# Expert rounds of 32 slots over all columns, with the third round in a TensorE branch

## The chip, the cores and the metric

One core of a Trainium2 chip runs the whole kernel as one program. The metric is the device time of that core in microseconds, and of several runs the median counts. TensorE does the matmuls (its sequencer fetches, waits and branches), VectorE (DVE), ScalarE (ACT) and GpSimd (POOL) work on rows of tiles, SyncE (SP) mostly issues DMAs; 16 DMA engines move the data for all of them.

## The reference

One decoder layer for 512 prompt tokens and 32 sample tokens (544 in all, `d_model` 1024, float32): a gated convolution and a forgetting attention, merged by sigmoid gates, a layer norm, then a routed mixture of 16 experts and a second layer norm. Only the mixture matters here:

```python
gl = (t @ w_group)                       # 4 groups, the best one is taken
el = (t @ w_router)                      # 4 experts in each group
top_w, top_i = lax.top_k(softmax(el of the best group), 2)
ids = g_idx * 4 + top_i                  # two experts a token
for e in range(16):
    h = silu(t @ w1[e]) * (t @ w3[e])    # 1024 -> 512
    y = y + gate[:, e:e + 1] * (h @ w2[e])   # 512 -> 1024
x = layer_norm(ALPHA * x + y)
```

Each of the 544 tokens goes to two experts, so an expert has 68 tokens on average.

## The kernel before, in words

The kernel first computes the two branches and the first layer norm, writes the normed rows to `x1d` in HBM, ranks the router's logits and gives every token a slot in its two experts' lists (L1078 to L1084). An expert has `CAP` = 96 slots; a block behind `tc.If(top > CAP)` (L1527), skipped here, does the rest if a list is longer.

**Weights.** All 16 experts' weights stream from HBM through a ring of 20 places of 1 MB (`RING`, `raw_load`, L778): per expert four `we` tiles (j = 0 to 3, each two rows k of w1 and of w3, two DMAs of 512 KB) and two `wd` tiles (j = 4, 5, each half of w2, one DMA). Nearly all are issued by SP's queue, in the order of use: up(e) first half, up(e) second half, down(e-1), up(e+1) and so on. From the 21st on, a load also waits until the tile five places before it has landed (L807 to L811, `AHEAD` = 5).

**One expert.** `place` (L1109) compares slots with list positions and takes token numbers and gates out by five matmuls, `gather` (L1119) fetches up to 96 rows of `x1d` by an indirect DMA on POOL. `x_t` (L1208) transposes them on VectorE, 12 instructions of 32x256 elements (expert 0 uses TensorE instead). `up` (L1229) forms x @ w1 and x @ w3, `glu` (L1238) the silu product, `h_t` (L1245) transposes h by 16 VectorE instructions of 32x96, `down` (L1266) forms h @ w2, scales by the gate (one ScalarE operation for columns 0 to 767, three of VectorE for the rest) and adds the rows into `acc` in HBM by an indirect DMA on POOL (L1279). For the last two experts (`E0` = 14 on) `down_kept` keeps y in SBUF instead and TensorE adds it at the end.

**How the matmuls are packed.** The stationary operand of a matmul is 32 slots, a quarter of TensorE's columns, so four matmuls run side by side in the four column groups q:

```python
for s in range(3):
    for q in range(4):
        g, c = (q, s) if q < 3 else (s, 3)
        mm(out(q, s), lhs(k, g), rhs(c), start=k == 0 and s != 1, ...)
```

g is a group of 32 slots, c a quarter of the output columns: column group q < 3 holds slots 32q to 32q+31 and quarters 0 to 2 in turn, group 3 holds quarter 3 of all slots. A *round* is one s: four matmuls of 256 moving columns. Up has 8 values of k with three rounds each, down 4.

**Order.** In the loop at L1318 the program order is up(e) first half, h_t(e-1), x_t(e+1), up(e) second half, place and gather of e+4, down(e-1), glu(e). Two double banks of PSUM alternate between up's and down's results. Before it (L1138 to L1196): lists of experts 0 and 1 and their gathers, then the arithmetic of the gates on VectorE, with matmuls on constants (`keep_warm`) that fill TensorE's gaps. After it: the residual rows are loaded from `x1d` by SP and `acc` is added onto them by POOL (L1357 to L1374), TensorE adds the kept experts (`z_part`), and the second layer norm follows in an order written out by hand (`TAIL`).

Of the kernel before, what the change touches and what calls it, by code (L numbers as in the profile page):

```python
# [33 lines left out]
NT = 5  # L34
# [54 lines left out]
def layer_kernel(ctx: ExitStack, tc: tile.TileContext, i_, o_):  # L89
# [18 lines left out]
    w1 = i_["w1"].rearrange("l e (p k) c -> p (l e) k c", p=128)  # L108
    w3 = i_["w3"].rearrange("l e (p k) c -> p (l e) k c", p=128)
# [839 lines left out]
    wk = []  # L949

    def parts_of(x, n, cm=None):
# [5 lines left out]
        if (x, n) == (NT - 1, 1):  # L957
            wk.append(ps_mm("wake")[:, 0])
            keep_warm(wk[0], WK[0])
# [120 lines left out]
    mm(pps[:, :NT * NE], before, asf.rearrange(flat), start=False, stop=True, skip_group_check=True)  # L1080
    keep_warm(wk[0], WK[3])
# [7 lines left out]
    gat3 = small("gat3", [NE, 3])  # L1089
# [50 lines left out]
    keep_warm(wk[0], WK[4])  # L1140

# [60 lines left out]
    def packed_mm(out, lhs, rhs, k, last):  # L1202
        for s in range(3):
            for q in range(4):
                g, c = (q, s) if q < 3 else (s, 3)
                mm(out(q, s), lhs(k, g), rhs(c), start=k == 0 and s != 1, stop=k == last, skip_group_check=True)  # L1206

    def x_t(e):  # L1208
        x = p2.tile([128, 8, CAP], F32, name="xgT", tag=("xgh", "xgl")[e % 2], bufs=1)
        if e:  # L1210
            rows = xgs[e % NXG].rearrange("c (p k) -> c k p", k=8)
            for g in range(3):
                for j in range(4):
                    nc.vector.transpose(x[32 * j:32 * j + 32, :, 32 * g:32 * g + 32],  # L1214
                                        rows[32 * g:32 * g + 32, :, 32 * j:32 * j + 32])
            return x
        for q in range(2):
            pp = (ps_t if q == 0 else ps_o)("xgT")
            for k in range(4):
                nc.tensor.transpose(pp[:, k, :CAP], xgs[e % NXG].rearrange("c (p k) -> c k p", k=8)[:CAP, 4 * q + k],  # L1220
                                    ident[:CAP, :CAP])
# [6 lines left out]

    def up(e, a, pab, x):  # L1229
        flat = pab.rearrange("p a b -> p (a b)")  # L1230
        for j in (2 * a, 2 * a + 1):
            raw = raw_e(e, j)
            for kk in range(2):
                packed_mm(lambda q, s: flat[32 * q:32 * q + 32, 256 * s:256 * s + 256].rearrange("p (a b) -> p a b", a=2),
                          lambda k, g: x[:, k, 32 * g:32 * g + 32],
                          lambda c: raw[:, :, kk, 128 * c:128 * c + 128], 2 * j + kk, 7)
# [8 lines left out]
    def h_t(su, tag="hh"):  # L1245
        h = p2.tile([128, 4, CAP], F32, name="hT", tag=tag, bufs=1)
        if tag == "hh":
            h3 = h[:, 3].rearrange("p (g c) -> p g c", g=3)
            for q in range(4):
                for j in range(4):  # L1250
                    ps = slice(32 * j, 32 * j + 32)
                    nc.vector.transpose(h[ps, :3, 32 * q:32 * q + 32] if q < 3 else h3[ps],  # L1252
                                        su[32 * q:32 * q + 32, :, 32 * j:32 * j + 32])
            return h
        pp = ps_t("hT")
        for k in range(3):
            nc.tensor.transpose(pp[:, k], su[:, k], ident)
        h_done.append((nc.scalar.activation(h[:, :3], pp[:, :3, :CAP], AF.Copy),
                       nc.vector.tensor_copy(h[:, 3].rearrange("p (g c) -> p g c", g=3), pp[:, :3, CAP:])))
# [5 lines left out]

    def down(e, h):  # L1266
        y = p2.tile([CAP, D], F32, name="y", tag="y", bufs=YB)
        py = ps_mm("py").rearrange("p a b -> p (a b)")
        for j in range(2):
            raw = raw_e(e, 4 + j)  # L1270
            for kk in range(2):
                packed_mm(lambda q, s: py[32 * q:32 * q + 32, 256 * s:256 * s + 256],
                          lambda k, g: h[:, k, 32 * g:32 * g + 32],
                          lambda c: raw[:, kk, 256 * c:256 * c + 256], 2 * j + kk, 3)
        nc.scalar.activation(y[:, :768], py[:CAP, :768], AF.Copy, scale=gat[:CAP, e:e + 1])  # L1275
        for s in range(3):
            nc.vector.tensor_scalar(y[32 * s:32 * s + 32, 768:], py[96:, 256 * s:256 * s + 256], gat3[96:, e, s:s + 1],
                                    None, op0=ALU.mult)
# [39 lines left out]
    for e in range(NE):  # L1318
        pab = ps_mm("pab")
# [22 lines left out]
        if e == NE - 1:  # L1342
            su = glu(pab)
            ht2 = h_t(su, "hl")
            with tc.issue_after(h_done[-1][0].ins):
# [181 lines left out]
    with tc.If(top > CAP):  # L1527
# [17 lines left out]
        with tc.For_i(0, NE, 1) as e:  # L1545
# [3 lines left out]
            for w in (w1, w3):  # L1549
                wt = halves_of("wt", [128, 1, 4, 512])  # L1550
                for a in range(2):
                    nc.sync.dma_start(wt[a], w[:, bass.ds(e, 1), 4 * a:4 * a + 4])
# [6 lines left out]
            for t in range(NT):  # L1559
# [4 lines left out]
                for q in range(2):  # L1564
                    pp = ps_t("xoT")
                    for k in range(4):
                        nc.tensor.transpose(pp[:, k, :m], xt.rearrange("c (p k) -> c k p", k=8)[:m, 4 * q + k],
# [3 lines left out]
                for i in range(2):  # L1571
                    for k in range(8):
                        mm(pab[:m, i], xT[:, k, :m], wup[i][k // 4][:, 0, k % 4], start=k == 0, stop=k == 7)
# [56 lines left out]
```

## Time and profile before

| | us |
|---|---|
| median of 3 runs | 770.4 (769.72 to 771.73) |
| the profiled execution, its own time | 777.0 |
| its span, first to last instruction | 775.3 |
| TensorE busy | 729.9 (94%) |
| VectorE busy | 478.8 (62%) |
| ScalarE busy | 200.6 (26%) |
| the expert stage, first up matmul to last down product | 471.6 to 745.8 |

The rows below come from the profiled execution, so terms of a sum are set against its 777.0 us. A line gives a start and a length in us, or for a group of instructions the busy time and the mean of one in ns; a name like pab<-we,xgT is the tile written and the tiles read, and Lnnn the line of the kernel. After an arrow stands what ended a wait.

### The profile page before, as it was taken

Reading aid. Unit: us, or ns where it says so; the run is one execution under the profiler, and the core shown is the slowest. Engines: PE = TensorE matmul, PEld = TensorE weight load, DVE = VectorE, ACT = ScalarE, POOL = GpSimd, SP = SyncE. Lnnn points to the kernel's source line nnn. Section 1 sums busy time; section 2 is a strip of 40 time slices with the busy share of each in tenths; the row PEclk is TensorE's granted clock in tenths of the full one; section 3 lists DMA queues with packets and bytes.
Section 4 is the critical chain, followed back from the end, with each engine's and each line's share of the span. In section 5 each row is a group of like instructions: output and inputs, shape, how many; then the busy total and the mean of one; then the engine's idle time right before and its main releaser. Section 6 shows DMA issues by size and latency. Waiting matters only on the chain.

```text
span 775.3 us, 18856 instructions
## 1 busy us (share of the span) xinstructions
PE 729.9 (94%) x8105; PEld 560.3 (72%) x8105; DVE 478.8 (62%) x1148; ACT 200.6 (26%) x360; POOL 131.7 (17%) x170
## 2 busy tenths in 40 slices
PE   7799999999999999999999977989999999999990
PEld 5599888899797999999976734545555555566550
DVE  3333766763345222333555776699999999986457
ACT  3343556534145222222424320001000010001132
POOL 5411000013441000000020531011111111100134
PEclk8899999999999999999999997999999999999995
DMA  9545411126543434434175697999999999999853
GB/s 231 168 151 183 129 59 56 59 65 208 163 119 106 163 114 158 164 109 164 55 278 213 191 411 233 332 343 354 358 367 361 342 357 346 351 377 362 318 119 117
DMA packets 65433, 169.66 MB, mean 219 GB/s; under 512 B 6145, under 2 KB 26673, under 8 KB 65345
## 3 DMA queue, kind: packets, MB, share of 16 engines
q1 hardware_dynamic: 54928, 137.93, 50.1%
q0 software_dynamic: 9552, 27.84, 13.3%
q10 hardware_dynamic: 864, 2.62, 0.9%
q8 instruction: 66, 1.08, 0.6%
q14 instruction: 23, 0.18, 0.1%
HBM read 157.40 MB, written 14.49 MB: 222 GB/s over the span
## 4 chain that ended last, share of the span: by engine, by line
PE 84%; DVE 7%; DMA 5%; issue 2%; ACT 1%; SPq 0%; DVEq 0%; another core or an unknown queue 0%; POOLq 0%; ACTq 0%
PE pab L1206 17%; PE pj L169 10%; PE pj L171 9%; PE pj L170 9%; PE py L1206 9%; DVE xgT L1214 3%; DMA xg<-x1d,gix 2%; PE py L171 2%; PE py L170 2%; PE py L169 2%; PE py L1288 2%; PE po L170 2%; PE po L171 2%; PE po L169 2%; PE S L567 1%
## 5 line engine op out<-in xcount | busy, mean ns | idle before, releaser
L1206 PE MATMUL pab<-we,xgT 128*32 128x256 f32 x3072 | 173.6, 385 | 4.8 <-DVE su L1242 4.8
L1206 PEld LDWEIGHTS pab<-we,xgT 128*32 128x32 f32 x3072 | 100.4, 112 | 73.7 <-DVE su L1242 5.3
L1214 DVE STREAM_TRANSPOSE xgT<-xg 32x256 f32<-32x256 f32 x180 | 115.7, 643 | 12.2 <-DMA xg<-x1d,gix 6.8
L1206 PE MATMUL py<-wd,hT 128*32 128x256 f32 x1344 | 76.6, 380 | 0.2 <-DVE hT L1252 0.2
L169 PE MATMUL pj<-xth,wgas 128*128 128x272 f32 x256 | 73.9, 288 | 0.0
L170 PE MATMUL pj<-xtl,wgas 128*128 128x272 f32 x256 | 73.8, 288 | 0.0
L171 PE MATMUL pj<-xth,wgas 128*128 128x272 f32 x256 | 73.6, 288 | 0.0
L165 DVE TENSOR_TENSOR wgas<-wga,wgas 128x1024 fp32r<-128x1024 f32 x16 | 19.6, 1226 | 85.6 <-ACT wgas L164 85.6
L1252 DVE STREAM_TRANSPOSE hT<-su 32x96 f32<-32x96 f32 x240 | 64.7, 269 | 7.9 <-PE py L1206 4.1
L1206 PEld LDWEIGHTS py<-wd,hT 128*32 128x32 f32 x1344 | 42.8, 110 | 28.3 <-DVE hT L1252 1.2
L1241 ACT ACTIVATE su<-pab 128x384 f32<-128x384 f32 x16 | 7.8, 490 | 170.8 <-DVE hT L1252 113.6
L169 PEld LDWEIGHTS pj<-xth,wgas 128*128 128x128 f32 x256 | 48.2, 188 | 0.8 <-issue 0.8
L170 PEld LDWEIGHTS pj<-xtl,wgas 128*128 128x128 f32 x256 | 48.1, 188 | 0.0
L171 PEld LDWEIGHTS pj<-xth,wgas 128*128 128x128 f32 x256 | 48.1, 188 | 0.0
L1279 POOL DMA_INDIRECT acc<-y,gix x14 | 20.1, 1434 | 163.2 <-DVE hT L1252 152.4
L169 PE MATMUL pj<-xth,wqks 128*128 128x272 f32 x128 | 38.6, 302 | 0.0
L171 PE MATMUL pj<-xth,wqks 128*128 128x272 f32 x128 | 36.9, 288 | 0.0
L170 PE MATMUL pj<-xtl,wqks 128*128 128x272 f32 x128 | 36.9, 288 | 0.0
L164 ACT ACTIVATE wgas<-wga 128x1024 fp32r<-128x1024 f32 x16 | 16.9, 1055 | 45.0 <-DMA wga<-in_w_in_dram 44.2
L1275 ACT ACTIVATE y<-py,gat 96x768 f32<-96x768 f32 x14 | 12.5, 896 | 60.8 <-PE py L1206 60.8
L170 PE MATMUL po<-wos,mxh 128*128 128x512 f32 x64 | 26.0, 406 | 0.4 <-DVE wos L165 0.4
L169 PE MATMUL po<-wos,mxl 128*128 128x512 f32 x64 | 25.5, 402 | 0.0
(442 smaller groups left out, 1553.5 us busy)
## 6 DMA issues: line engine op xcount, KB each, us to landing
we<-in_w_dram SPq DMA_DIRECT2D x124, 512.0 KB
wd<-in_w_dram SPq DMA_DIRECT2D x31, 1024.0 KB
wga<-in_w_in_dram SPq DMA_DIRECT2D x8, 1024.0 KB
wqk<-in_w_in_dram SPq DMA_DIRECT2D x4, 1024.0 KB
wo<-in_w_o_dram SPq DMA_DIRECT2D x4, 1024.0 KB
xa<-in_x_prompt_dram SPq DMA_DIRECT2D x4, 512.0 KB
ckb<-cdr POOLq DMA_DIRECT2D x8, 256.0 KB
wcg<-in_w_in_dram SPq DMA_DIRECT2D x2, 1024.0 KB
```

The source lines that it names most:

```text
L164: nc.scalar.activation(h, src, AF.Copy)
L165: (eng or nc.vector).tensor_sub(l, src, h.bitcast(F32))
L169: mm(out, al, bh, start=first, stop=False)
L170: mm(out, ah, bl, start=False, stop=False)
L171: return mm(out, ah, bh, start=False, stop=last)
L1206: mm(out(q, s), lhs(k, g), rhs(c), start=k == 0 and s != 1, stop=k == last, skip_group_check=True)
L1214: nc.vector.transpose(x[32 * j:32 * j + 32, :, 32 * g:32 * g + 32], rows[32 * g:32 * g + 32, :, 32 * j:32 * j + 32])
L1241: nc.scalar.activation(su, ab[:, :, 0], AF.Silu)
L1252: nc.vector.transpose(h[ps, :3, 32 * q:32 * q + 32] if q < 3 else h3[ps], su[32 * q:32 * q + 32, :, 32 * j:32 * j + 32])
L1275: nc.scalar.activation(y[:, :768], py[:CAP, :768], AF.Copy, scale=gat[:CAP, e:e + 1])
L1279: nc.gpsimd.indirect_dma_start(out=acc, out_offset=bass.IndirectOffsetOnAxis(ap=gix[:CAP, e:e + 1], axis=0), in_=y, in_offset=None, bounds ...
L1288: pe_last.append(mm(py[:CAP], h[:, k], raws[k // 2][:, k % 2, n * 512:(n + 1) * 512], start=k == 0, stop=k == 3))
```

## The change

Slots are taken in three rounds of 32 (g = 0, 1, 2), and in a round the four column groups hold the four quarters of the up columns. The quarters are interleaved in blocks of 32 columns, so that one VectorE transpose by 32x32 blocks turns h over whole. Down has its four column groups hold slots 0 to 63 in two halves of the columns (rounds 0 and 1) or slots 64 to 95 in four quarters (round 2). For experts 0 to 13 the third round stands in a branch of TensorE on a bit that says whether the expert has more than 64 tokens; the bits are counted by five matmuls, packed by VectorE and loaded into a register of TensorE. Both PSUM banks become lasting tiles, and ScalarE sets the third round's columns of up to zero once. The y scalings all go to ScalarE, w1 and w3 are cut so that a piece is contiguous in HBM, and x's rows are taken in the matching order. The overflow block is adapted and otherwise as before.

```diff
-    w1 = i_["w1"].rearrange("l e (p k) c -> p (l e) k c", p=128)
+    w1 = i_["w1"].rearrange("l e (j p r) c -> p (l e) j r c", p=128, r=2)
...
-            return [2, 2, 512], [(w[:, e, 2 * j:2 * j + 2], i) for i, w in enumerate((w1, w3))]
+            return [2, 2, 512], [(w[:, e, j], i) for i, w in enumerate((w1, w3))]
...
+    full = ps_s("full")
+    for x in range(NT):
+        mm(full[:, :NE], onesb, asf[:, x], start=x == 0, stop=x == NT - 1)
     keep_warm(wk[0], WK[3])
...
         if e < E0:
-            for s in range(3):
-                nc.vector.tensor_copy(gat3[96:, e, s:s + 1], gat[32 * s:32 * s + 32, e:e + 1])
+            nc.scalar.activation(gat2[64:, e, 0:1], gat[:64, e:e + 1], AF.Copy)
+            for q in range(4):
+                nc.scalar.activation(gat2[32 * q:32 * q + 32, e, 1:2], gat[64:96, e:e + 1], AF.Copy)
...
     second = place_early(1)[1]
     keep_warm(wk[0], WK[4])
+    bits = p2.tile([1, NE], F32, name="bits")
+    many = p2.tile([1, 2], F32, name="many")
+    manyi = p2.tile([1, 1], I32, name="manyi")
+    for e in range(NE):
+        nc.gpsimd.memset(bits[:, e:e + 1], float(2 ** e))
+    nc.vector.scalar_tensor_tensor(bits, full[:1, :NE], 64.0, bits, op0=ALU.is_gt, op1=ALU.mult,
+                                   accum_out=many[:, 0:1])
+    nc.vector.tensor_copy(manyi, many[:, 0:1])
+    third_of = nc.values_load(manyi[:1, 0:1], engines=[mybir.EngineType.PE], min_val=0, max_val=2 ** NE - 1)
...
+    def rows_by_two(xr):
+        return xr.rearrange("c (j p r) -> c j r p", p=128, r=2)
...
-                    nc.vector.transpose(x[32 * j:32 * j + 32, :, 32 * g:32 * g + 32],
-                                        rows[32 * g:32 * g + 32, :, 32 * j:32 * j + 32])
+                    nc.vector.transpose(x[32 * j:32 * j + 32, :, 32 * g:32 * g + 32].rearrange("p (j r) s -> p j r s", r=2),
+                                        rows[32 * g:32 * g + 32, :, :, 32 * j:32 * j + 32])
...
+    def up_round(g, pab, x, raws, ks):
+        out = pab.rearrange("p a b -> p (a b)")[:, 256 * g:256 * g + 256].rearrange("p (a b f) -> p a b f", a=2, f=32)
+        for k in ks:
+            rhs = raws[k // 2][:, :, k % 2].rearrange("p a (b c f) -> p a b c f", c=4, f=32)
+            for c in range(4):
+                mm(out[32 * c:32 * c + 32], x[:, k, 32 * g:32 * g + 32], rhs[:, :, :, c], start=k == 0 and g != 1,
+                   stop=k == 7, skip_group_check=True)
+    banks.append(ps_mm("moe"))
+    for b in banks:
+        nc.scalar.activation(b[:, 1, :256], ident.unsqueeze(1).to_broadcast([128, 2, 128]), AF.Copy, scale=0.0)
...
+    def third(e):
+        return tc.If((third_of >> e) & 1 > 0) if e < E0 else ExitStack()
     def up(e, a, pab, x):
-        for j in (2 * a, 2 * a + 1):
-            raw = raw_e(e, j)
-            for kk in range(2):
-                packed_mm(..., 2 * j + kk, 7)
+        raws = {}
+        ks = range(4 * a, 4 * a + 4)
+        for k in ks:
+            if k % 2 == 0:
+                raws[k // 2] = raw_e(e, k // 2)
+            for g in range(2):
+                up_round(g, pab, x, raws, (k,))
+        with third(e):
+            up_round(2, pab, x, raws, ks)
...
     def h_t(su, tag="hh"):
         h = p2.tile([128, 4, CAP], F32, name="hT", tag=tag, bufs=1)
-        if tag == "hh":
-            h3 = h[:, 3].rearrange("p (g c) -> p g c", g=3)
-            for q in range(4):
-                for j in range(4):
-                    ...
-        pp = ps_t("hT")
-        for k in range(3):
-            nc.tensor.transpose(pp[:, k], su[:, k], ident)
+        h_done.append(nc.vector.transpose(h.rearrange("p b (g s) -> p g b s", g=3),
+                                          su.rearrange("p g (b f) -> p g b f", b=4)))
+        return h
...
+    def down_round(r, py, h, raws, ks):
+        for k in ks:
             for q in range(4):
+                g, c = (q % 2, 2 * (q // 2) + r) if r < 2 else (2, q)
+                mm(py[32 * q:32 * q + 32, 256 * r:256 * r + 256], h[:, k, 32 * g:32 * g + 32],
+                   raws[k // 2][:, k % 2, 256 * c:256 * c + 256], start=k == 0 and r != 1, stop=k == 3,
+                   skip_group_check=True)
     def down(e, h):
+        for j in range(2):
+            raws[j] = raw_e(e, 4 + j)
+            for k in (2 * j, 2 * j + 1):
+                for r in range(2):
+                    down_round(r, py, h, raws, (k,))
+        with third(e):
+            down_round(2, py, h, raws, range(4))
-        nc.scalar.activation(y[:, :768], py[:CAP, :768], AF.Copy, scale=gat[:CAP, e:e + 1])
-        for s in range(3):
-            nc.vector.tensor_scalar(y[32 * s:32 * s + 32, 768:], py[96:, 256 * s:256 * s + 256], gat3[96:, e, s:s + 1],
-                                    None, op0=ALU.mult)
+        nc.scalar.activation(y[:64, :512], py[:64, :512], AF.Copy, scale=gat[:64, e:e + 1])
+        nc.scalar.activation(y[:64, 512:], py[64:, :512], AF.Copy, scale=gat2[64:, e, 0:1])
+        for q in range(4):
+            nc.scalar.activation(y[64:, 256 * q:256 * q + 256], py[32 * q:32 * q + 32, 512:768], AF.Copy,
+                                 scale=gat2[32 * q:32 * q + 32, e, 1:2])
...
     for e in range(NE):
-        pab = ps_mm("pab")
+        pab = bank()
```

## Rows read from the trace of the kernel before

**Rows 1.** The chain of waits, 540 to 600: start, us, what

```profile
552.45 5.32 PE py L1206 x96
557.76 10.36 PE pab L1206 x192
568.12 0.32 PE pmt L1113 x5
```

**Rows 2.** Windows: busy us of PE, PEld, DVE, ACT, POOL; PEclk, DMA share, GB/s

```profile
440.00:460.00 20.00, 18.39 (x116) 10.56 (x114) 15.57 (x55) 5.55 (x9) 6.53 (x5) 1.00 0.99 374
...
480.00:500.00 20.00, 19.95 (x362) 11.67 (x358) 12.56 (x44) 0.98 (x2) 3.43 (x3) 1.00 1.03 334
500.00:550.00 50.00, 45.00 (x782) 25.57 (x778) 48.39 (x117) 3.67 (x5) 5.91 (x5) 0.97 1.00 355
550.00:600.00 50.00, 50.00 (x919) 29.71 (x911) 48.13 (x125) 4.16 (x6) 8.41 (x7) 1.00 1.01 361
```

**Rows 3.** Waits of SP's queue, 472 to 550: us, times, longest

```profile
SPq L805 <- PE pab L1206: 28.9, 12, 8.4
SPq L805 <- PE pmt L1113: 24.6, 4, 17.8
SPq L805 <- PE py L1206: 11.4, 5, 3.3
```

**Rows 4.** Waits of SP's queue, 550 to 718

```profile
SPq L805 <- DMA we<-in_w_dram: 78.6, 38, 4.7
SPq L805 <- DMA wd<-in_w_dram: 44.2, 17, 5.0
SPq L805 <- PE pab L1206: 1.4, 4, 0.4
```

**Rows 5.** Timeline of SP's queue, 712 to 725: start, us, instructions

```profile
713.84 4.54 SPq L805 DMA_DIRECT2D wd<-in_w_dram  x2
718.49 3.62 SPq L1365 DMA_DIRECT2D z<-x1d  x3
```

**Rows 6.** Timeline, 735 to 746: start, us, instructions, idle before

```profile
736.34 0.91 POOL L1374 DMA_DIRECT2D z<-acc  x1 [13.95 <-DMA z<-x1d]
...
738.64 4.46 PE L1288 MATMUL py<-wd,hT 128*96 128x512 f32 x10
...
744.23 0.67 DVE L1426 SCALAR_TENSOR_TENSOR z<-z,pz 128x512 f32<-128x512 f32 x1
```

**Rows 7.** Timeline, 460 to 525

```profile
461.41 1.06 POOL L1120 DMA_INDIRECT xg<-x1d,gix  x1 [6.11 <-DVE pg L1162]
...
471.57 7.76 PE L1206 MATMUL pab<-we,xgT 128*32 128x256 f32 x96
...
507.13 12.23 PE L1206 MATMUL pab<-we,xgT 128*32 128x256 f32 x192 [4.84 <-DVE su L1242]
```

**Rows 8.** Windows, after TensorE's gap before 507

```profile
507.00:510.50 3.50, 3.37 (x32) 1.58 (x36) 3.37 (x9) 0.00 (x0) 0.85 (x1) 0.52 0.93 371
```

**Rows 9.** One line's instructions: L1352, L1527 (ns min/median/max)

```profile
L1352 PEldq TENSOR_LOAD <-flagi x1: 485/485/485, 751.3 to 751.3; - x1
...
L1527 PEldq COMPARE_BRANCH  x1: 3589/3589/3589, 751.9 to 751.9; - x1
...
L1527 DVEq COMPARE_BRANCH  x1: 76/76/76, 770.9 to 770.9; - x1
```

**Rows 10.** Groups of instructions, 480 to 720: busy us, mean ns, idle

```profile
L1214 DVE STREAM_TRANSPOSE xgT<-xg 32x256 f32<-32x256 f32 x171 | 109.9, 643 | 12.1 <-DMA xg<-x1d,gix 6.8 <-PE pab L1206 2.8
...
L1252 DVE STREAM_TRANSPOSE hT<-su 32x96 f32<-32x96 f32 x232 | 62.5, 269 | 7.8 <-PE py L1206 4.1
...
L1277 DVE TENSOR_SCALAR y<-py,gat 32x256 f32<-32x256 f32 x42 | 20.6, 490 | 0.6
...
L1275 ACT ACTIVATE y<-py,gat 96x768 f32<-96x768 f32 x14 | 12.5, 896 | 60.8 <-PE py L1206 60.8
...
L1241 ACT ACTIVATE su<-pab 128x384 f32<-128x384 f32 x15 | 7.4, 490 | 165.8 <-DVE hT L1252 113.6 <-PE pab L1206 52.2
```

More of the change, by code (lines that the diff above doesn't have):

```diff
@@ L948, in layer_kernel @@
     zt_last = {}
-    wk = []
+    wk, banks = [], []
     def parts_of(x, n, cm=None):
@@ L1088, in layer_kernel @@
     gat = small("gat", [NE])
-    gat3 = small("gat3", [NE, 3])
+    gat2 = small("gat2", [NE, 2])
     gix = small("gix", [NE], I32)
@@ L1196, in layer_kernel @@
     nc.vector.tensor_copy(flagi[:1], flag[:1])
-    def packed_mm(out, lhs, rhs, k, last):
-        for s in range(3):
-            for q in range(4):
-                g, c = (q, s) if q < 3 else (s, 3)
-                mm(out(q, s), lhs(k, g), rhs(c), start=k == 0 and s != 1, stop=k == last, skip_group_check=True)
+    def rows_by_two(xr):
+        return xr.rearrange("c (j p r) -> c j r p", p=128, r=2)
     def x_t(e):
@@ L1219, in x_t @@
             for k in range(4):
-                nc.tensor.transpose(pp[:, k, :CAP], xgs[e % NXG].rearrange("c (p k) -> c k p", k=8)[:CAP, 4 * q + k],
+                nc.tensor.transpose(pp[:, k, :CAP], rows_by_two(xgs[e % NXG])[:CAP, 2 * q + k // 2, k % 2],
                                     ident[:CAP, :CAP])
@@ L1264, in layer_kernel @@
     pe_last = []
+    def down_round(r, py, h, raws, ks):
[5 more added lines that the diff above has]
+                   skip_group_check=True)
     def down(e, h):
         y = p2.tile([CAP, D], F32, name="y", tag="y", bufs=YB)
[L1268 removed]
+        py = bank().rearrange("p a b -> p (a b)")
+        raws = {}
         for j in range(2):
[L1270 to L1274, printed above, removed]
[L1275 to L1278 removed]
+            raws[j] = raw_e(e, 4 + j)
[6 more added lines that the diff above has]
+        nc.scalar.activation(y[:64, 512:], py[64:, :512], AF.Copy, scale=gat2[64:, e, 0:1])
+        for q in range(4):
+            nc.scalar.activation(y[64:, 256 * q:256 * q + 256], py[32 * q:32 * q + 32, 512:768], AF.Copy,
+                                 scale=gat2[32 * q:32 * q + 32, e, 1:2])
         nc.gpsimd.indirect_dma_start(out=acc, out_offset=bass.IndirectOffsetOnAxis(ap=gix[:CAP, e:e + 1], axis=0),
@@ L1344, in layer_kernel @@
             ht2 = h_t(su, "hl")
-            with tc.issue_after(h_done[-1][0].ins):
+            with tc.issue_after(h_done[-1].ins):
                 onehots_t(e)
@@ L1566, in layer_kernel @@
                     for k in range(4):
-                        nc.tensor.transpose(pp[:, k, :m], xt.rearrange("c (p k) -> c k p", k=8)[:m, 4 * q + k],
+                        nc.tensor.transpose(pp[:, k, :m], rows_by_two(xt)[:m, 2 * q + k // 2, k % 2],
                                             ident[:m, :m])
@@ L1572, in layer_kernel @@
                     for k in range(8):
-                        mm(pab[:m, i], xT[:, k, :m], wup[i][k // 4][:, 0, k % 4], start=k == 0, stop=k == 7)
+                        mm(pab[:m, i], xT[:, k, :m], wup[i][k // 4][:, 0, k % 4 // 2, k % 2], start=k == 0, stop=k == 7)
                 su = p2.tile([128, 512], F32, name="suo", tag="su", bufs=1)
```

26 lines of the change are left out of this document (10 added, 16 removed).

## The prediction, made before the changed kernel ran

> **What bounds the kernel now.** The engine table says only who is busy over the span: TensorE most, VectorE next. The chain of waits says where: in the expert stage every piece of it belongs to TensorE, one expert after another [rows 1]. A period is 10.36 (up) + 0.32 (placing) + 5.32 (down) = 16.0 us, with no gap between the pieces. Up is 96 matmuls, recorded as 192 (two passes each), in 24 rounds of four blocks: 10.36 / 24 = 0.432 us a round. Down has 12 rounds.
>
> Behind TensorE stands a second bound, which the windows show: from 480 to 600 the DMA engines are busy 1.00 to 1.03 of the time, at 334 to 361 GB/s [rows 2]. By the code one expert's weights are eight pieces of 512 KB and two of 1024 KB, 6.29 MB. At 355 GB/s they take 17.7 us, more than the 16.0 us in which TensorE uses them up, and gathers and accumulating scatters share the engines. The kernel can do this because the ring has 20 places of 1 MB and is full when the experts begin. The waits of SP's queue show that stock run down: from 472 to 550 weight loads wait for TensorE to free a place (28.9 + 24.6 + 11.4 us) [rows 3], from 550 to 718 for earlier loads to land (78.6 + 44.2 us) and hardly for TensorE (1.4 us in its largest group) [rows 4]. At the end little is left: the last two weight tiles are issued from 713.84 on, the last one just before the transfer at 718.49 [rows 5]. The code lets a load go when the one five tiles before it has landed, so five tiles are under way: 5 x 1.05 MB / 355 GB/s = 14.8 us, and the last lands near 733 (an estimate from these rows). TensorE comes to that tile one block after 738.64, at about 739.5 [rows 6]: the stock is then worth 6.5 us. **TensorE is the bound, and the delivery of weights lies only some 6 us behind it.**
>
> **The change part by part.**
>
> *Rounds left out.* An expert of at most 64 tokens skips slots 64 to 95: 8 of 24 rounds up and 4 of 12 down, 12 x 0.432 = 5.18 us. The reference's router, worked out on its own inputs (seed 0), gives experts 0 to 15 the counts 63 58 79 72 54 64 63 69 67 57 64 58 82 84 69 85. Of the 14 that can branch, 8 skip (0, 1, 4, 5, 6, 9, 10, 11); 2, 3, 7, 8, 12 and 13 keep all rounds behind a branch, 14 and 15 without one. TensorE loses 8 x 5.18 = 41.5 us of work.
>
> *What of this reaches the end.* Little: from 550 on loads already follow one another through full DMA engines [rows 2, 4], and a faster TensorE adds no bytes per second. It waits for weights instead. What moves is the beginning. The first half of expert 0 takes 7.76 us [rows 7]; with 8 of 12 rounds it is over 7.76 / 3 = 2.6 us sooner, and loading, which stood still on a full ring (the longest single wait is 17.8 us [rows 3]), resumes that much earlier. After it, until 550, loads no longer wait for places: 20 us at 334 and 50 us at 355 GB/s go at 361 [rows 2], 20 x (1 - 334/361) + 50 x (1 - 355/361) = 2.3 us. So weights end 4.9 us sooner. The lower bound is 0 (all of it lost to gathers, which then come earlier too), the upper one 4.9 plus the 6.5 us of stock, if the tail follows the last tile.
>
> *The tail.* Since TensorE then waits for the last tile and not the tile for TensorE, up to 6.5 us more can go. But the end needs the residual rows too: POOL, after 13.95 us of waiting for a load, issues the accumulation onto the first of them at 736.34, and VectorE adds to that row at 744.23 [rows 6]. This chain moves with the DMA queue, by 4.9 us, not with TensorE. Its landing stands in no row and lies between the two times, so between 0 and 6.5 us go; I take the middle, 3.3.
>
> *The branches*, three per branching expert, 42. VectorE's taken branch cost 0.076 us; TensorE's only one took 3.589 us, and it jumps over the whole overflow loop [rows 9]. Here 16 matmuls are jumped over. I take 0.1 us, since that distance is nearer to VectorE's, and keep 3.6 for a rival. At 0.1 us, 4 us in all, TensorE's new waiting covers it; without that cover it would count in full.
>
> The Trainium skill's page "Runtime: NRT & Kernel Launch" (section "Instruction fetch mechanics") speaks against this part: a taken branch whose target lies outside the fetched window has to load the target's page first, so control flow at run time is dear. By that rule, should every skip be such a miss, the time would be rival C's. The trace's long TensorE jump agrees with it; no run here shows a short one on TensorE.
>
> *Counting and the register.* Five matmuls of 16 columns (five small ones take 0.32 us [rows 1]), two small VectorE operations (each under the 0.27 us of the smallest transpose [rows 10], 0.5 us in all), 16 one-element memsets on POOL, which waited 6.11 us before the first gather [rows 7], and a register load on TensorE, 0.485 us [rows 9]. TensorE has little but warming matmuls there until the gathered rows land, shortly before its first up matmul at 471.57 [rows 7], so only VectorE's part lies on the way to the gates: +0.5 us. Were the memsets queued behind the gathers, VectorE would stand before the gate arithmetic, with everything behind it on its queue, and TensorE's gate products behind that: up to 2 us, kept for the range.
>
> *VectorE and ScalarE.* The 16 transposes of h (269 ns each, 4.3 us) become one of 128x384: forms of 96 and 256 columns give (643 - 269) / 160 = 2.34 ns a column, 269 + 288 x 2.34 = 943 ns [rows 10]; the upper bound is the 4.3 us of now. Three scalings of y (490 ns) leave VectorE. ScalarE's one of 896 ns becomes six: by the forms of 768 and 384 columns 1.06 ns a column, 2.7 us [rows 10], with five copies of one column more. ScalarE works 4 us in 50 in this stage [rows 2], so it covers this at nothing; if it did not, y's scatter would be late. VectorE is nearly full now (48 of 50 us [rows 2]); without these 4.8 us per expert TensorE's gain could not be used before 550. The 12 transposes of x keep count and size; another stride may make them cheaper, or up to twice as dear (12 x 0.643 = 7.7 us more), which fits into the time that weights take per expert.
>
> *Order of w1 and w3.* Pieces stay as many and 4 KB a row; their place in HBM becomes contiguous, as w2's already is. Taken as 0; the bounds are the 334 and 374 GB/s of neighbouring windows [rows 2].
>
> *Later release.* The third round reads both tiles of a half, so the first is freed with the second. It costs nothing where loads wait for landings, and the 2.6 us at the start already count both as freed together.
>
> **Sum.** 4.9 + 3.3 - 0.5 = 7.7 us. The profiled execution's own time becomes 777.0 - 7.7 = 769.3; that execution is 6.6 us above the median of the runs shown, so against the median it is 770.4 - 7.7 = **762.7 us**.
>
> **The rivals.**
> *A, weights arrive faster.* If the new order of w1 and w3 lets loading run at the 374 GB/s of 440 to 460 rather than 355 [rows 2], 255 us of it shrink by 255 x (1 - 355/374) = 13 us: 750. If delivery were no bound at all, 770.4 - 41.5 = 729. Against it: the DMA engines are full, and the contiguous w2 already is a third of the bytes. 0.08.
> *B, no change.* The gain turns into waiting. The residual rows may be just in time, so that the tail gives nothing; and a TensorE that waits runs slower afterwards: after a gap of 4.84 us [rows 7] the next 3.5 us were granted 0.52 of the clock, 1.2 GHz for most of them [rows 8], which loses 1.7 us of work. Three such gaps near the end take the 4.9 us back: 770. Against it: experts 12 to 15 run all rounds, 16.0 us of work where weights take 17.7 and more, so gaps there are short. 0.17.
> *C, slower: branches stall.* Each skip costs what TensorE's one branch did: 24 x 3.589 = 86 us against the 41.5 saved, 770.4 + 44.6 = 815. It decides from 41.5 / 24 = 1.7 us per skip on. Against it: that branch jumps over a loop many times longer. 0.10.
> *D, it skips nothing*, because the block is entered anyway: 770 to 774. The counts speak against it. 0.03, two parts of three for no change.
>
> **How the numbers follow.** The forecast has 0.62; its own range goes from 756 (4.9 + 6.5, and some faster delivery) to 767 (half the early gain and no tail). What a measurement of this kernel can tell from no change is about 0.3%, 2.3 us. Faster: 0.62 + 0.08 = 0.70; the same: 0.17 + 0.02 = 0.19; slower: 0.10 + 0.01 = 0.11. The range 753 to 773 leaves out C and most of A.
>
> **What would show it.** Right: TensorE's periods of about 11 us for the first skipping experts, and from about expert 10 on gaps before up pieces that weight transfers end; SP's waits for TensorE gone after 480, those for landings there from the start; DMA share 1.0 as before; the last weight tile issued near 713; one h transpose of about 0.9 us. Wrong: branches of microseconds on TensorE, more than 375 GB/s from 500 to 700, or a last tile issued no earlier than now.

## The result, and the profile after

The changed kernel takes 776.1 us in the median of six runs (773.7 to 777.5), the kernel before 770.7 in runs beside them (768.5 to 771.8). The ratio is 1.0070, with a 95% interval of 1.0048 to 1.0092: **slower by 0.7%**, where 1% faster was forecast, and outside the forecast range. The profiled execution takes 775.7 us, with a span of 774.0.

The spans of the two traces, 775.3 before and 774.0 after, do not show the loss, because the profiled execution of the kernel before came late to the expert stage: its first up matmul starts at 471.57 [rows 7], the changed kernel's at 465.84. From there to the end of the last down product it is 274.2 us before and 278.9 after, so times of the two traces are best compared from these starts.

Inside the expert stage the rounds are skipped as forecast. First the page's busy times, then TensorE's timeline:

```profile
PE 701.7 (91%) x7339; PEld 549.8 (71%) x7339; DVE 359.6 (46%) x842; ACT 247.5 (32%) x501; POOL 133.1 (17%) x186
```

```profile
465.84 5.82 PE L1247 MATMUL moe<-we,xgT 128*32 128x256 f32 x64
...
472.36 3.66 PE L1247 MATMUL moe<-we,xgT 128*32 128x256 f32 x64
...
476.49 3.66 PE L1247 MATMUL moe<-we,xgT 128*32 128x256 f32 x64
...
485.73 3.66 PE L1295 MATMUL moe<-wd,hT 128*32 128x256 f32 x64
...
491.67 10.57 PE L1247 MATMUL moe<-we,xgT 128*32 128x256 f32 x192 [2.28 <-DVE su L1278]
```

A half of up without its third round is 64 records and 3.66 us; half of expert 2's 192 records in 10.57 us is 5.3. TensorE's busy time falls from 729.9 to 701.7 us and VectorE's from 478.8 to 359.6. SP's waits between 472 and 550 changed hands too; columns: us, times, longest:

```profile
SPq L805 <- DMA we<-in_w_dram: 33.5, 17, 3.8
SPq L805 <- DMA wd<-in_w_dram: 17.8, 7, 3.9
SPq L805 <- PE pmt L1118: 13.6, 2, 13.4
SPq L805 <- PEq L1271: 6.2, 2, 3.9
```

In [rows 3] TensorE held SP there for 64.9 us; now it is mostly landings. Weights come no faster, as one window shows, first before and then after; the last two columns are DMA share and GB/s:

```profile
500.00:700.00 200.00, 195.00 (x3538) 115.32 (x3534) 190.27 (x470) 16.64 (x24) 28.11 (x23) 0.99 1.00 356
```

```profile
500.00:700.00 200.00, 174.18 (x2968) 109.45 (x2963) 84.06 (x207) 53.02 (x125) 27.74 (x22) 0.98 1.01 356
```

Nor do they come sooner: the four `we` loads of the last up half start 236.5 us after the first up matmul in both (at 708.09 before, at 702.32 after).

The loss is at the end of SP's queue. Its timeline, for comparison with [rows 5], and then the chain of waits:

```profile
702.32 3.39 SPq L805 DMA_DIRECT2D we<-in_w_dram  x4
706.16 4.14 SPq L1401 DMA_DIRECT2D z<-x1d  x3
717.59 0.78 SPq L1408 DMA_DIRECT2D z<-acc  x2
718.43 1.31 SPq L805 DMA_DIRECT2D wd<-in_w_dram  x2
```

```profile
709.64 7.94 DMA acc<-y,gix
717.58 0.02 issue
717.59 0.32 SPq L1408
...
718.95 19.36 DMA wd<-in_w_dram
738.31 0.04 issue
738.36 3.67 PE py L1324 x8
```

Before, the last two weight tiles (wd) were issued ahead of the residual loads. Now five residual loads stand ahead of them, and the fourth reads `acc`: it waits for the last scatter, issued at 709.64 and landed 7.94 us later. From 705.7 to 718.4 no weight load was issued, and the last tile went out at 718.95, 253.1 us after the first up matmul (before: at 718.00, 246.4 us after it). TensorE, which began expert 14's down product 245.2 us after the first up matmul (before: 249.9), waited for both tiles:

```profile
732.16 3.73 PE L1324 MATMUL py<-wd,hT 128*96 128x512 f32 x4 [3.92 <-DMA wd<-in_w_dram]
738.36 3.67 PE L1324 MATMUL py<-wd,hT 128*96 128x512 f32 x8 [2.47 <-DMA wd<-in_w_dram]
...
742.82 1.88 PE L1324 MATMUL py<-wd,hT 128*96 128x512 f32 x4
```

No line of the diff orders these DMAs: in the text of both kernels the residual loads stand ahead of the last two tiles (L1400 and L1489 before, L1436 and L1525 after). Each queue's order is made when the program is built, and it came out differently.

### The profile page after: what moved, and what is told of

It reads as the page before. It is cut to its first block, busy times and chain, and to the rows that moved or that the text cites. A ratio compares the mean times of both kernels' runs of the same rounds, so it can differ in the third digit from the quotient of the medians.

```text
span 774.0 us, 17319 instructions
## 1 busy us (share of the span) xinstructions
PE 701.7 (91%) x7339; PEld 549.8 (71%) x7339; DVE 359.6 (46%) x842; ACT 247.5 (32%) x501; POOL 133.1 (17%) x186
## 5 line engine op out<-in xcount | busy, mean ns | idle before, releaser
L1247 PE MATMUL moe<-we,xgT 128*32 128x256 f32 x2560 | 151.9, 387 | 19.6 <-DMA we<-in_w_dram 11.8
L1247 PEld LDWEIGHTS moe<-we,xgT 128*32 128x32 f32 x2560 | 96.1, 111 | 72.5 <-issue 31.5
L1227 DVE STREAM_TRANSPOSE xgT<-xg 32x256 f32<-32x256 f32 x180 | 78.3, 435 | 109.3 <-PEq L1271 50.4
L1295 PE MATMUL moe<-wd,hT 128*32 128x256 f32 x1088 | 65.5, 388 | 10.0 <-DMA wd<-in_w_dram 7.4
L1295 PEld LDWEIGHTS moe<-wd,hT 128*32 128x32 f32 x1088 | 36.2, 111 | 35.3 <-issue 9.3
L1277 ACT ACTIVATE su<-moe 128x384 f32<-128x384 f32 x16 | 7.8, 490 | 110.7 <-PE moe L1247 61.9
L1125 POOL DMA_INDIRECT xg<-x1d,gix x16 | 16.7, 1046 | 92.3 <-DVE gix L1112 51.0
L846 ACT ACTIVATE sg<-pj 128x544 f32<-128x544 f32 x16 | 9.9, 617 | 55.4 <-PE pj L171 54.5
L1310 ACT ACTIVATE y<-moe,gat 64x512 f32<-64x512 f32 x14 | 9.5, 682 | 55.4 <-PEq L1308 18.7
```

The costliest lines, as they stand in the source:

```text
L846: nc.scalar.activation(h2(e), pm, AF.Sigmoid)
L1125: return nc.gpsimd.indirect_dma_start(out=xgs[e % NXG][:CAP], out_offset=None, in_=x1d, in_offset=bass.IndirectOffsetOnAxis(ap=gix[:CAP, e ...
L1247: mm(out[32 * c:32 * c + 32], x[:, k, 32 * g:32 * g + 32], rhs[:, :, :, c], start=k == 0 and g != 1, stop=k == 7, skip_group_check=True)
L1295: mm(py[32 * q:32 * q + 32, 256 * r:256 * r + 256], h[:, k, 32 * g:32 * g + 32], raws[k // 2][:, k % 2, 256 * c:256 * c + 256], start=k == ...
L1310: nc.scalar.activation(y[:64, :512], py[:64, :512], AF.Copy, scale=gat[:64, e:e + 1])
```

## The experiments

Sixteen runs, four at a time on one chip. Each ratio is to the kernel before on the same chip, over five rounds. Absolute times move between the groups (before: 771.4, 778.2, 770.8 and 770.8 us; in the traces of the second group the first up matmul starts at 471.7 to 473.6, in those of the others at 460.8 to 467.7), and the two kernels that ran twice came out 0.23 and 0.24% apart in ratio, so neighbours of one group are compared first, and an expectation in us is read by its ratio to 770.7.

| run | what | median us | ratio (95%) |
|---|---|---|---|
| e1 | changed, wd tiles first | 765.4 | 0.9911 (0.9881 to 0.9942) |
| e2 | changed, no branches | 773.2 | 1.0040 (1.0017 to 1.0063) |
| e3 | all rounds, no branches | 767.9 | 0.9959 (0.9939 to 0.9979) |
| e4 | before, residual loads first | 778.9 | 1.0102 (1.0081 to 1.0123) |
| e5 | no branches, wd first | 769.2 | 0.9879 (0.9856 to 0.9902) |
| e6 | every branch entered, wd first | 772.7 | 0.9922 (0.9898 to 0.9945) |
| e7 | before, new row order alone | 773.5 | 0.9936 (0.9914 to 0.9958) |
| e8 | as e5, skipping 0 and 1 only | 773.2 | 0.9934 (0.9911 to 0.9956) |
| e9 | e7, VectorE loaded early | 767.6 | 0.9962 (0.9937 to 0.9988) |
| e10 | e7, VectorE loaded late | 765.2 | 0.9921 (0.9895 to 0.9948) |
| e11 | e1, twice the branches | 765.2 | 0.9939 (0.9915 to 0.9963) |
| e12 | e1 again | 766.3 | 0.9934 (0.9912 to 0.9956) |
| e13 | as e5, skipping 4 to 11 only | 767.7 | 0.9961 (0.9942 to 0.9979) |
| e14 | e5 again | 762.1 | 0.9903 (0.9880 to 0.9925) |
| e15 | e5, places freed late | 763.8 | 0.9918 (0.9894 to 0.9942) |
| e16 | no branches in 0 and 1, then branches | 763.4 | 0.9904 (0.9879 to 0.9929) |

**The order at the end: e1 to e4.** e1 takes the tiles of the last expert from the ring before the residual loads and puts these behind them:

```diff
+    raws = down_raws(NE - 1)
     for x in range(NT):
         z_load(x)
...
-        nc.sync.dma_start(z, x1d[t * 128:t * 128 + m, :])
+        with tc.issue_after(loads[-1].ins):
+            nc.sync.dma_start(z, x1d[t * 128:t * 128 + m, :])
```

(the two loads from `acc` likewise). e4 does the reverse to the kernel before:

```diff
-    raws = down_raws(e)
+    with tc.issue_after(z_last[-1].ins):
+        raws = down_raws(e)
```

e2 replaces `with third(e):` by `if e not in SKIP:` with the eight experts written out; e3 runs every round:

```diff
-        return tc.If((third_of >> e) & 1 > 0) if e < E0 else ExitStack()
+        return ExitStack()
```

> The changed kernel with one thing moved: the last two weight tiles are issued on SP ahead of the residual loads, as in the kernel before. Theory O (SP's order at the end is the loss: in the changed kernel the last weight tile is issued at 718.95 us behind a residual load that waits for the last scatter, and TensorE waits for it until 738.36): the two tiles are issued between 706 and 712, the last lands near 728, the residual rows then land some 4 to 8 us later than now, and the time is 766 to 770 us, 1.2% or so below the changed kernel. Theory B (branches: 29.4 + 9.3 us of TensorE's waits stand at 'issue'): the time stays at 774 to 777 us. Theory D (the weights as a whole come no sooner and TensorE's waiting costs its clock): 773 to 777 us, with the same end.

> The changed kernel without any branch: the rounds of slots 64 to 95 are left out of the program for the eight experts that have at most 64 tokens in this input, and stand in line for the others. SP's order at its end is that of the changed kernel, residual loads ahead of the last two weight tiles. Theory O: 774 to 777 us, no faster than the changed kernel, since the order at the end is the same. Theory B: the branches go, 24 skips and 18 entries of up to 2 to 3 us in the places where the trace shows waits at 'issue', so 765 to 771 us. Theory D: 773 to 777 us.

> The changed kernel with all rounds run by every expert and no branch, so that the new tiling, the new order of w1 and w3 and the lighter VectorE stand alone; SP's order at its end is that of the kernel before (last weight tiles ahead of the residual loads). Theory O: 767 to 771 us, as the kernel before or a little faster. Theory B: the same, 767 to 771 us, since there is no branch. A third theory, that the new forms themselves (transposes, six evictions, order of the weights) cost the time: 774 to 778 us.

> The kernel before with one thing moved: its last two weight tiles are issued on SP behind the residual loads, as in the changed kernel. Theory O: the tiles go from 713.84 to where the last scatter has landed, 728 us or later, so TensorE's last part starts 8 to 14 us later than 738.64, and the time is 778 to 786 us. Theory B and theory D: the order is of no account, 769 to 773 us.

Theory O held in all four: read by the ratios, 763.8, 773.8, 767.5 and 778.6 us (e1 2.2 and e2 0.2 us below their ranges). Moving the tiles back turns 1.0070 into 0.9911, 1.6%; moving them away from the kernel before costs 1.0%. SP's timeline and TensorE's last products in e1:

```profile
702.40 3.40 SPq L805 DMA_DIRECT2D we<-in_w_dram  x4
707.56 2.98 SPq L805 DMA_DIRECT2D wd<-in_w_dram  x2
710.64 3.58 SPq L1402 DMA_DIRECT2D z<-x1d  x3
717.84 1.33 SPq L1410 DMA_DIRECT2D z<-acc  x2
```

```profile
728.15 4.46 PE L1324 MATMUL py<-wd,hT 128*96 128x512 f32 x10
...
733.38 1.88 PE L1324 MATMUL py<-wd,hT 128*96 128x512 f32 x4
```

The `we` loads before are issued within 0.1 us of the changed kernel's. Only the two tiles move, both by over 8 us; the last product ends at 735.3 instead of 744.7 (270.4 us after the first up matmul instead of 278.9), and the span ends at 764.5 instead of 774.0. In e4 the chain shows the changed kernel's wait:

```profile
715.09 7.96 DMA acc<-y,gix
724.38 18.46 DMA wd<-in_w_dram
742.87 5.37 PE py L1288 x8
```

Two rivals fall here. Branches are not the loss: without any (e2) the kernel is still slower than before, and the step from 1.0070 to 1.0040 lies within the intervals. Nor are they the reason for the order: e2 has no branch and the changed kernel's order at SP's end, e3 runs all rounds and has the old one. e2 and e3 differ only in the rounds left out of the program, so leaving rounds out is enough to move the order; the changed kernel has all rounds in its program, a part of them in blocks, and its order moved too. How the builder weighs this was not looked into.

**Price and worth of the branches: e5, e6, e11, e12.** e5 is e2 with e1's order; e6 is e1 with `64.0` replaced by `0.0` in the comparison that sets the bits, so every block is entered; e11 is e1 with each block split:

```diff
-        with third(e):
-            up_round(2, pab, x, raws, ks)
+        for h in (ks[:2], ks[2:]):
+            with third(e):
+                up_round(2, pab, x, raws, h)
```

> The run without branches (rounds left out of the program for the eight experts) with the last two weight tiles ahead of the residual loads. In the traces so far the four weight loads of the last up half end on SP 246.7 us (changed kernel) and 247.9 us (tiles moved) after the first gather with branches, 245.4 us with all rounds, and 240.5 us without branches. Theory E (the gain at the start, 4.9 us in the forecast, is real, and the branches lose it again between 465 and 500 us, where loads still wait for TensorE): 758 to 763 us, 4 to 6 us below the 765.4 of the branched kernel with the same order. Theory F (the 240.5 is a chance of one profile; weights come at the same time whatever TensorE does): 764 to 768 us.

> The branched kernel with the last two tiles moved, and the bound on the count set from 64 to 0, so that every branch falls through into its rounds: the blocks stay, nothing is skipped. Beside the run with all rounds and no blocks (767.85 us) it gives the price of the blocks, beside the skipping one (765.4 us) what the skipping is worth. Theory E: the blocks cost 4 to 7 us at the start, so 771 to 775 us. Theory F: blocks at 0.2 us each lie beside waits for weights, 767 to 769 us.

> The branched kernel with the last two tiles ahead of the residual loads, each branch split in two: 84 branches on TensorE instead of 42, the same rounds left out. Beside the next run, on the same chip. Theory E (the blocks eat the gain of the skipping, some 3 to 4 us): 3 to 4 us more, so 0.994 to 0.997 of the kernel before. Theory F (a branch costs the 0.2 us of most of TensorE's branch rows, beside waits): at most 1.5 us more.

> The branched kernel with the last two weight tiles ahead of the residual loads a second time, as the measure for the doubled branches, and because its interval (0.9881 to 0.9942) does not yet tell it from the run in which every branch is entered (0.9922) nor from the one without branches (0.9879). If the branched skipping is worth what the skipping without branches is worth: 0.986 to 0.989. If the branches eat it: 0.991 to 0.994.

Doubling the branches moved the ratio by 0.0005: theory F. In e6 blocks that are entered cost nothing beside e3 either: 0.9922, where e3 has 0.9959 and theory E wanted over 1.000. TensorE's branch instructions in the changed kernel, min/median/max in ns: the first three, all skips, and then all of up and of down:

```profile
L1271 PEldq COMPARE_BRANCH  x3: 215/221/243, 470.2 to 478.9; - x3
```

```profile
L1271 PEldq COMPARE_BRANCH  x40: 67/184/2075, 470.2 to 679.2; - x40
```

```profile
L1308 PEldq COMPARE_BRANCH  x20: 68/180/3324, 488.0 to 704.5; - x20
```

A skip takes some 0.22 us where the forecast took 0.1, and what comes near the 3.6 us of [rows 9] is a rare maximum. What the long ones waited for shows in the DMA packets: the longest, from 488.03 to 491.35, ends 2.5 us after a transfer of 16 KB has begun on queue q8, which carries instructions. Below are q8's packets, MB and share in that branch, then in the whole changed kernel and in e14, which has no branches:

```profile
q8 instruction: 1, 0.02, 2.0%
```

```profile
q8 instruction: 66, 1.08, 0.6%
```

```profile
q8 instruction: 60, 0.98, 0.5%
```

The 3.589 us of [rows 9] end 2.5 us after such a transfer has begun too, and in all eighteen traces every branch row of TensorE over 0.9 us ends 2.3 to 2.8 us after one. That q8 is TensorE's is worked out from the counts: both kernels execute 7339 matmul records, but e14 has 768 of them and their weight loads fewer in its program, 1536 instructions, or 256 for each of the six transfers. So skipped instructions are loaded all the same. The Trainium skill, page "Runtime: NRT & Kernel Launch", section "Instruction fetch mechanics", would make a skip dear where its target's page has to be loaded first. The traces agree for the few long ones; most branches here paid no such price.

TensorE's waits listed as "issue", which looked like the branches' price (31.5 and 9.3 us before L1247 and L1295 in the changed kernel), stand in e2 without a branch too:

```profile
PEld moe L1248 <- issue: 31.9, 56, 4.3
...
PEld moe L1296 <- issue: 7.1, 9, 2.1
```

But with branches the skipping is worth nothing that can be seen: 0.9911 and 0.9934 with it, 0.9922 with every block entered. Without branches it is worth something: e5 is 3.6 us below e6 on the same chip, and e14 repeats it (0.9903).

**Where skipping counts: e8, e13 to e16.** e8 and e13 are e5 with `SKIP` cut to (0, 1) and to the other six. e15 moves the second round of each half's first tile to the end of the half (and the same in down), so that its ring place comes free late, as with a branch. e16 is e1 with `if e > 1:` ahead of each block, so that experts 0 and 1 always leave their rounds out.

> No branches, last two tiles first, and only experts 0 and 1 leave their rounds out: 10.4 us less of TensorE's work instead of 41.5. Forecast's step (what reaches the end is the sooner restart of loading in the first experts; later skipping turns into waiting): the time of the run that leaves out all eight, within 1.5 us. If the skipping of experts 4 to 11 mattered: 3 us or more above it, towards the 767.85 of all rounds. Theory F: the same as all rounds, 766 to 769.

> No branches, last two tiles first, rounds left out for experts 4, 5, 6, 9, 10 and 11 but not for 0 and 1. Theory of the forecast (what reaches the end is the first experts' sooner restart of loading): no gain over the kernel with all rounds, 0.992 to 0.996 of the kernel before. Theory G (the later skipping carries it): as the next run, within 0.2%.

> The run without branches that leaves out the rounds of all eight experts, a second time, as the measure for its two neighbours. 0.986 to 0.990 if its first value (0.9879) was no chance; 0.991 to 0.994 if skipping is worth nothing however it is made.

> The same run with the second round of the first tile's rows moved to the end of each half in the eight experts, so that a ring place comes free only with the half's end, as with the branches. Theory R (the earlier release carries the gain of the run without branches): 3 us or more slower than its neighbour, 0.991 to 0.994. Otherwise within 1.5 us of it.

> Experts 0 and 1 without branches and without their rounds, branches from expert 2 on, last two tiles first. In the traces the branched kernels take 27 to 28 us from the first up matmul of expert 0 to that of expert 2, those without branches 23, with every branch entered 29. Theory E2 (the loss of the branches lies there): as the run without branches, 0.986 to 0.990. Otherwise 0.991 to 0.994, as the branched kernel.

The first two experts alone give little or nothing (e8 beside e6 and e7: 773.2, 772.7, 773.5 us), the later six alone little or nothing (0.9961, beside e3's 0.9959). Both together give 5.5 us over the six alone (767.7 to 762.1) and 4.0 us over the two alone (773.2 to 769.2). So the forecast's step is half right: the sooner start is worth its 4.9 us, but only without branches and where TensorE keeps ahead of the weights later on. The traces agree: counted from the first up matmul, the last weight tile is issued at 245.3 us with all rounds (e3), at 244.3 with every block entered (e6), at 245.3 and 243.5 with skipping branches (e1, e12), and at 241.4 and 239.8 without branches (e5, e14). That one bound stands behind the other is argued from these runs; no trace shows the handover.

e15 lies 1.7 us above its neighbour e14, between the values expected in us and by its ratio (0.9918) inside theory R's range, with overlapping intervals: not decided. e16 (0.9904) stands with e14 (0.9903), just outside what theory E2 expects, and its timeline says why the branched kernel may lose there. From the first up matmul of expert 0 to that of expert 2 e16 takes 488.37 - 465.74 = 22.6 us, e12 494.78 - 467.74 = 27.0. In e12 the second half of expert 1 breaks off at its 59th record:

```profile
482.03 3.61 PE L1247 MATMUL moe<-we,xgT 128*32 128x256 f32 x59 [0.30 <-PEq L1271]
488.07 0.96 PE L1247 MATMUL moe<-we,xgT 128*32 128x256 f32 x5 [2.43 <-issue]
489.65 4.62 PE L1295 MATMUL moe<-wd,hT 128*32 128x256 f32 x64
```

The changed kernel breaks off at the same record (0.56 us there). Both gaps end 2.6 us after a transfer of q8 has begun (485.51 in e12, 482.03 in the changed kernel), so TensorE waited for instructions; with the branch of 1.54 us behind e12's down product this is most of the 4.4 us between e12 and e16. But in these traces they do not reach the end: from the first up matmul to the end of the last product e16 takes 268.3 us, e12 268.6 and e14 266.2. e16's interval (0.9879 to 0.9929) also overlaps e12's (0.9912 to 0.9956), and they ran in different groups. So the stall is shown, and whether it costs the kernel time is open.

**Row order and VectorE: e7, e9, e10.** e7 gives the kernel before the two `rearrange` lines of w1 and w3, the matching `piece_of` and `rows_by_two` in `x_t`, nothing else. e9 and e10 add to it, for experts 1 to 3 or from 6 on:

```diff
+            if e in range(1, 4):
+                for g in range(2):
+                    for j in range(3):
+                        nc.vector.transpose(...)
```

with the operands of the transpose above it, so six of the twelve are done twice.

> The kernel before with the new row order of w1 and w3 alone (each piece contiguous in HBM, the gathered rows transposed with the other stride). If the 3 to 4 us by which the run with all rounds lies below the kernel before come from the row order (faster weights or VectorE's cheaper transposes, 643 to 435 ns): 766 to 769 us. If they come from the lighter VectorE and TensorE's steadier start instead: 769.5 to 772.5 us, no difference that can be measured. Only the second half of the gain would be settled: the first value does not tell the weights from the transposes, which the trace then does by GB/s between 480 and 700 us.

> The run with the new row order alone (ratio 0.9936) with six transposes of 0.435 us done twice for experts 1 to 3, 2.6 us of VectorE's time per expert, what the cheaper transposes (643 to 435 ns, 12 an expert) had given back there. Theory V (the gain of the row order comes over VectorE: in the kernel before TensorE stood 4.84 us at 507 for VectorE's product of silu and then ran slow, in the run with the new order 1.78 us, and until 550 loads wait for TensorE): that gap returns to 4 us or more and the ratio to 0.997 to 1.001. Theory L (contiguous pieces arrive faster): the ratio stays at 0.992 to 0.995 though TensorE has the gap.

> The same with the six repeated transposes for experts 6 to 15 alone, ten times 2.6 us of VectorE's time and none before 550 us. Theory V: VectorE has the room there, since TensorE takes 16.0 us an expert and weights 17.7: the ratio stays at 0.992 to 0.996. If VectorE's load counts wherever it falls: 0.997 or more.

The row order alone is worth 0.64%, 4.9 us, most of what the whole change gives with its tail mended. VectorE's transposes of x for expert 2, first in the kernel before, then in e7, and TensorE's next up product in e7:

```profile
498.06 7.13 DVE L1214 STREAM_TRANSPOSE xgT<-xg 32x256 f32<-32x256 f32 x11
```

```profile
496.82 4.92 DVE L1217 STREAM_TRANSPOSE xgT<-xg 32x256 f32<-32x256 f32 x11
```

```profile
503.50 10.57 PE L1206 MATMUL pab<-we,xgT 128*32 128x256 f32 x192 [1.78 <-DVE su L1245]
```

In [rows 7] TensorE waited 4.84 us at this place for VectorE's product `su`, which stands behind those transposes in its queue, and then took 12.23 us at a lower clock [rows 8]; e4, the same kernel up to there, repeats it with 4.84 and 12.05. Here it waits 1.78 and takes 10.57. With the repeated transposes early (e9) a gap (3.17 us, where 4 or more was expected) and the slow product are back, and the ratio rises to 0.9962, just short of the range expected; late (e10) it stays at 0.9921. TensorE in e9, then the windows after the gap in e7 and in e9 (the third number from the end is the granted clock):

```profile
497.31 13.37 PE L1206 MATMUL pab<-we,xgT 128*32 128x256 f32 x192 [3.17 <-DVE su L1250]
```

```profile
503.50:507.00 3.50, 3.50 (x67) 2.12 (x71) 3.38 (x10) 0.00 (x0) 0.72 (x1) 1.00 1.02 405
```

```profile
497.30:500.80 3.50, 3.49 (x36) 1.65 (x40) 3.29 (x10) 0.00 (x0) 0.73 (x1) 0.50 0.98 385
```

Why this counts, the chain of waits in the kernel before says: from 472 to 520 it is mostly VectorE's, and TensorE's only from there on.

```profile
505.86 0.53 DVE xgT L1214
506.62 0.47 DVE su L1242
...
520.08 0.28 DVE hT L1252
520.40 5.16 PE py L1206 x90
```

Afterwards TensorE works without a break (from 500 to 700 it is busy 195.00 of 200 us before and 200.00 in e9), so what it loses early it does not win back. From the first up matmul to the end of the last product e7 takes 267.8 us, e10 267.9, e9 272.2 and the kernel before 274.2, while two traces of one kernel differ by 1.8 (e1 and e12, e5 and e14). The loss does not run over the loads: the last four `we` loads start 235.0 us after the first up matmul in e7 and 234.8 in e9.

So the traces speak for theory V. The times only lean to it: the step from e10 to e9 (2.3 us in the medians) is little more than half an interval's width, and 0.9962 lies between the ranges of theories V and L. Of theory L the windows leave little, 356 GB/s before, 359 in e7 and 357 in e9 from 500 to 700; but no run took the contiguous pieces alone.

## Why the prediction was wrong, step by step

**The step that failed** is the one behind both *What of this reaches the end* and *The tail*: that the end "moves with the DMA queue" and the queue keeps its order, "the last weight tile issued near 713" ahead of the residual loads, as in [rows 5]. The queue's order did not stay. The tile was issued at 718.95, behind a load that waits for the last scatter. That costs 1.4 to 1.6% (1.0070 against 0.9934 and 0.9911), 10 to 12 us. Of the forecast's own signs of being wrong it is the third, "a last tile issued no earlier than now". The sum counted only what the diff moves.

With the old order the sign and nearly the size are right: e1 and e12 are 0.9 and 0.7% faster, 6.9 and 5.1 us where 7.7 was forecast. That nearness is luck, because the terms were not these:

- *Rounds left out*: the count is right. Up and down have 3648 records left (below) of 4416, 768 fewer, which is 96 rounds. Their busy time falls from 250.2 to 217.4 us, by 32.8 and not 41.5: a round takes 217.4 / 456 = 0.477 us on average, before 250.2 / 552 = 0.453.

```profile
L1247 PE MATMUL moe<-we,xgT 128*32 128x256 f32 x2560 | 151.9, 387 | 19.6 <-DMA we<-in_w_dram 11.8
...
L1295 PE MATMUL moe<-wd,hT 128*32 128x256 f32 x1088 | 65.5, 388 | 10.0 <-DMA wd<-in_w_dram 7.4
```

- *What of this reaches the end*, 4.9: 5.5 us without branches and with all eight experts skipping (e13 to e14), nothing measurable with the branches as they are (e6 against e1 and e12; the last weight loads come 236.5 us after the first up matmul, before and after). This is a second step that failed.
- *The tail*, 3.3: in e1 the last product ends 735.3 - 710.2 = 25.1 us after the last tile's issue began, before 745.8 - 718.0 = 27.8, so 2.7. The residual rows were not the limit: from the last product to the end of the span it is 29.5 us before, 29.3 after and 29.2 in e1.
- *VectorE and ScalarE*, counted at nothing: mis-sized. "In the expert stage every piece of it belongs to TensorE" holds for the chain from 520 on; before that it is mostly VectorE's. The prediction had the 4.84 us gap in [rows 7] and used it only for a rival; it did not ask what VectorE's relief does to that gap. Row order and transposes alone give 4.9 us (e7).
- *The transposes*: one of h takes 0.578 us, forecast 0.943; those of x 0.435 instead of 0.643, which the forecast named as possible and counted at nothing. y's six scalings take 2 x 0.68 + 4 x 0.46 = 3.2 us on ScalarE, forecast 2.7, and are covered as said.
- *The branches*: some 0.2 us each where 0.1 was forecast; rival C is refuted by e11. What they cost beyond that are waits for instructions, some 4 us of them in the first two experts (e12 against e16), and whether these reach the end is open.
- *Counting and the register*, 0.5: from the first gather to the first up matmul it is 10.2 us before and after, so the term does not show. *Later release*, nothing: not decided (e15).
- *Order of w1 and w3*: from 500 to 700 us it is 356 GB/s before and after, so rival A did not come about.
- *Rival B* came nearest in outcome, by another way: the gain was lost, and more, at one wait in SP's queue.

## What to carry to other kernels

Before costing a change, ask which orders it leaves to the builder. Leaving out work on one engine can reorder another's queue (e2 against e3), and a queue that issues in order passes one late wait to all behind it; where an order matters (last weights ahead of loads that wait for results), write it down. Then read the chain of waits through the whole stage, its first experts too, and look for the engine behind each gap of the bounding engine; here the chain of a later stretch hid that VectorE set the pace before 520. With e1's order the change is 0.7 to 0.9% faster than the kernel before, and the row order alone gives 0.6%. The kernels that gain more (e5, e14, e16) leave rounds out by the counts of this one input and do not serve another.

## What the runs showed of the hardware

- A VectorE transpose of 32x256 elements took 643 ns when each 32x32 block's 32 source columns lay eight elements apart, and 435 ns with them two apart; one of 128x384 in single blocks took 578 ns, 16 of 32x96 took 16 x 269.
- TensorE's skips over 16 matmuls took 0.215 to 0.243 us in the first three rows, but its longest branch row among the experts 3.3 us. Every branch row over 0.9 us ended 2.3 to 2.8 us after a 16 KB instruction transfer had begun, and the instructions of skipped blocks were loaded too (66 transfers, 60 without them in the program).
- After an idle gap of 1.78 us (e7) TensorE's next 192 records took 10.57 us, at a granted clock of 1.00 (2.4 GHz) in the first 3.5 us; after 3.17 (e9) and 4.84 us (before) 13.37 and 12.23, at 0.50 and 0.52 (1.2 GHz for all or most of them). The gap's length alone does not decide: after 2.28 us in the changed kernel they took 10.57, after 2.02 us in e14 12.25.
